# A hybrid decoder block: the products with w_out and w_up by Strassen's algorithm too, and h normalised with tokens on partitions

## The chip, the cores and the metric

The kernel runs on one core of a Trainium2 chip. The metric is the device time of one execution in microseconds (us); lower is better. Three executions of the kernel before took 1032.06, 1034.04 and 1034.89 us, with a median of 1034.04 us.

## The reference

One layer, 512 tokens, width 1024, float32. `u = rmsnorm(x)`, one wide projection of `u`, a gated DeltaNet branch and a forgetting-attention branch with 8 heads each, their outputs merged by two sigmoid gates, and then the part that the change touches:

```python
merged = jax.nn.sigmoid(gate_a) * y_a + jax.nn.sigmoid(gate_b) * y_b
h = x + merged @ w_out[l]                                            # 1024 x 1024

hn = rmsnorm(h, norm_mlp_g[l])
x = h + jnp.square(jax.nn.relu(hn @ w_up[l])) @ w_down[l]            # 1024 x 4096, 4096 x 1024
```

## The kernel before

**Precision.** Every large product is made of three TensorE matmuls: each operand is split into a rounded part hi and a rest lo, and hi·hi, hi·lo and lo·hi are added in PSUM.

**Weight units.** All weights come in units of 128 x 1024. `seq` lists them in the order of use. For each unit `prefetch_raw` issues the load (SP's queue), LA_RAW = 3 units ahead of the call that uses it, and `prefetch_split` makes two tiles of it, LA_SPLIT = 2 units ahead: ScalarE casts hi (L185), VectorE subtracts (lo = raw - hi, L186). The pool `whl` has four buffers for hi and four for lo, so a unit's cast can start only when TensorE has used the hi of the unit four places before it. For most weights a unit is one call of `dense` (L197 to L208), which makes 128 outputs for all 512 tokens: 16 matmuls of 128x512 with hi (L203, L204), then 8 with lo (L207).

**w_out and w_up before.** They are eight and 4 x 8 such calls. After each w_out unit VectorE adds x (L913: h, features on partitions); ScalarE and VectorE split h times the norm's gain, and square and sum it. The reciprocal root of the mean square is computed by two sets of small matmuls (`sumsq` L282, `inv_rms` L294), spread over the partitions as `rb_h`, and multiplied in only behind the product with w_up (`relu`, L951; ScalarE squares, L952). So no step of the norm stands between the products with w_out and w_up. 32 transposes (`tokens_first`, L935) give h with tokens on partitions for the sum of the output.

**w_down before.** The 4096 features are taken in four chunks, each w_up (8 units) and then w_down. w_down is multiplied by Strassen's algorithm in Winograd's form: seven products P1, P5, P6, P3, P7, P2, P4 of half-size blocks instead of eight, each of two units (s0, s1) of 12 matmuls 128x512 (L1015 to L1017). The sums of weight blocks are made by DMA: P1, P3 and P2 use blocks as they are, and P5 = P1 + block, P6 = P5 + block, P4 = P6 + block, P7 = P3 + block are accumulating transfers on GpSimd's queue into the same tile (L161). Such a transfer can start only when the older sum has been split: TensorE's next-but-one product hangs on a chain split, transfer, split, transfer. The sums of activation blocks are `act_forms`, made by VectorE (L974 to L980) and split by ScalarE and VectorE (`shi` L968, `slo` L969). VectorE adds the products to the accumulators (L992).

**The order.** The code is written in program order; a scheduler then puts the instructions into one in-order queue for each engine by priorities and its own estimate of times. An instruction whose input is late holds everything behind it on its engine.

Of the kernel before, what the change touches and what calls it, by code (L numbers as in the profile page):

```python
# [23 lines left out]
NPG = 34  # L24
# [3 lines left out]
NDRAW = 7  # L28
NWARM = 10
NZ1 = 5  # L30
LA_RAW = 3
LA_SPLIT = 2
INV_STEP = 2500


def hybrid_block(tc, a, out):
# [4 lines left out]
    up = ctx.enter_context(tc.tile_pool(name="up", bufs=1))  # L41
# [3 lines left out]
    pmm = ctx.enter_context(tc.tile_pool(name="pmm", bufs=NMM, space=PSUM))  # L45
    pat = ctx.enter_context(tc.tile_pool(name="pat", bufs=8 - NMM, space=PSUM))
    drp = ctx.enter_context(tc.tile_pool(name="drp", bufs=1, space=DRAM))
    mix = ExitStack()
    rwp = mix.enter_context(tc.tile_pool(name="rwp", bufs=3))
    atp = mix.enter_context(tc.tile_pool(name="atp", bufs=1))  # L50
    sbp = mix.enter_context(tc.tile_pool(name="sbp", bufs=1))
    fxp = mix.enter_context(tc.tile_pool(name="fxp", bufs=2))

# [17 lines left out]

    def const(shape, s, dt=F32):
        return cp.tile(shape, dt, tag=s, name=s)
# [56 lines left out]
    for i in range(KT):  # L130
        seq += [("w_gb", i), ("w_pf", i)]
    seq += [("w_o", i) for i in range(KT)]
# [4 lines left out]
    PRODUCTS = ("P1", "P5", "P6", "P3", "P7", "P2", "P4")  # L137
    for c in range(NC):
        seq += [("w_u", c * 8 + i) for i in range(8)]
        seq += [(p, (c, s_)) for p in PRODUCTS for s_ in range(NSUB)]  # L140
    raws, units = [], []
    pos = [0]

    FACTOR = {"P1": (0, None), "P5": (1, "P1"), "P6": (2, "P5"), "P3": (2, None), "P7": (1, "P3"), "P2": (3, None),
              "P4": (3, "P6")}
    factors = {}

    def prefetch_raw(n):
        while len(raws) < min(len(seq), n):
            nme, i = seq[len(raws)]
            if nme in PRODUCTS:
                q, old = FACTOR[nme]
                if old is None:
                    raw = draw.tile([P, D], F32, tag="draw", name=nm("draw"))
                    nc.sync.dma_start(raw, a["w_d"][i[0], q, i[1]])
                else:
                    raw = factors[old, i[1]]  # L160
                    nc.gpsimd.dma_start(raw, a["w_d"][i[0], q, i[1]], accum_op=ALU.add)  # L161
                factors[nme, i[1]] = raw
                raws.append((raw, [slice(0, D)]))
                continue
            w = 256 if nme == "w_ab" else D
            raw = wraw.tile([P, D], F32, tag="raw", name=nm("raw"))
            cuts = [slice(0, 512), slice(512, D)] if 0 < len(raws) < 3 else [slice(0, w)]
            for c in cuts:
                nc.sync.dma_start(raw[:, c], a[nme][i][:, c])
            raws.append((raw, cuts))  # L170
# [18 lines left out]
    def unit(nme):  # L189
        n = pos[0]  # L190
        assert seq[n][0] == nme, (seq[n], nme)
        pos[0] += 1
        prefetch_raw(n + 1 + LA_RAW)
        prefetch_split(n + 1 + LA_SPLIT)
        return units[n]
# [101 lines left out]
    uhi = up.tile([P, KT, T], F32R, tag="uhi", name="uhi")  # L297
    ulo = up.tile([P, KT, T], F32R, tag="ulo", name="ulo")
# [9 lines left out]
    def uh(k):  # L308
        return uhi[:, k, :]

    def ul(k):
        return ulo[:, k, :]
# [468 lines left out]
    def fox_pair(hp):  # L781
        vts = ([], [])
        for pn in range(3):
            us = [unit("w_fox"), unit("w_fox")]
            pg2 = [page(s="fqk"), page(s="fqk")]
            for t2 in range(2):
                ps = mmps("fx")
                for tb in (2 * t2, 2 * t2 + 1):
                    o = ps[:, (tb % 2) * 256:(tb % 2 + 1) * 256]
                    for k in range(KT):  # L790
                        w = us[k // 4][0][:, (k % 4) * 256:(k % 4 + 1) * 256]
                        mm(o, uhi[:, k, cs(tb)], w, start=(k == 0), stop=False)  # L792
                        mm(o, ulo[:, k, cs(tb)], w, start=False, stop=False)  # L793
                    for k in range(KT):
                        mm(o, uhi[:, k, cs(tb)], us[k // 4][1][:, (k % 4) * 256:(k % 4 + 1) * 256], start=False,  # L795
                           stop=(k == KT - 1))
# [97 lines left out]
    mg = []  # L894
    for n in range(KT):
        ps = dense("w_gb", uh, ul)
        sg = page(s="sg")
        act.activation(sg, ps, AF.Sigmoid)
        ps = dense("w_pf", lst(obs, 0), lst(obs, 1))
        vec.tensor_tensor(sg, ps, sg, op=ALU.mult)  # L900
        pool.tensor_tensor(sg, sg, ma[n], op=ALU.add)
        mg.append(split(sg))


    hT, hg = [], []
    hhi = up.tile([P, KT, T], F32R, tag="uhi", name="hhi")
    hlo = up.tile([P, KT, T], F32R, tag="ulo", name="hlo")
    sqs = page(s="sqs")
    for n in range(KT):
        xi = row_tile(a["xT"][n])  # L910
        ps = dense("w_o", lst(mg, 0), lst(mg, 1))
        xr = page(s="h")
        vec.tensor_tensor(xr, ps, xi, op=ALU.add)  # L913
        hT.append(xr)
        hg.append(split(xr, mlp_g[:, n:n + 1], dst=(hhi[:, n, :], hlo[:, n, :])))
        sq = page(s="sq") if n else sqs
        act.activation(sq, xr, AF.Square)
        if n:
            vec.tensor_tensor(sqs, sqs, sq, op=ALU.add)
    rs_h = const([P, NCH], "rs_h")  # L920
    rb_h = const([P, T], "rb_h")
    start(inv_rms(sumsq(sqs), rs_h, rb_h))


    mix.close()
    draw = ctx.enter_context(tc.tile_pool(name="draw", bufs=NDRAW))
    actp = ctx.enter_context(tc.tile_pool(name="actp", bufs=2))
    accs = [None] * 8

    def tokens_first():  # L930
        for tb in range(NCH):
            for l in range(2):
                pt = atps("hT")
                for n in range(4):
                    nc.tensor.transpose(pt[:, cs(n)], hT[4 * l + n][:, cs(tb)], ident)  # L935
                acc = page(s="acc")
                act.copy(acc, pt)
                accs[tb * 2 + l] = acc
                yield

    def mlp_up(c):
        forms = []
        for s_ in range(NSUB):
            blocks = []
            for j in range(2):
                blk = actp.tile([P, 2, T], F32, tag="act", name=nm("act"))
                for f in range(2):
# [4 lines left out]
                    act.activation(blk[:, f, :], r, AF.Square)  # L952
                blocks.append(blk)
            forms.append(act_forms(*blocks))
        return forms

    def halves(x):
        return v3(x[:, :], 2)

    def act_forms(b0, b1):  # L960

        h_ = T // 2
        a11, a21, a12, a22 = b0[:, :, :h_], b0[:, :, h_:], b1[:, :, :h_], b1[:, :, h_:]
        res = {}

        def put(p, x):
            hi, lo = page(F32R, "shi"), page(F32R, "slo")
            act.copy(halves(hi), x)  # L968
            vec.tensor_tensor(halves(lo), x, halves(hi).bitcast(F32), op=ALU.subtract)  # L969
            res[p] = hi, lo  # L970
# [125 lines left out]
```

## Time and profile before

| | |
|---|---|
| median of three runs | 1034.04 us (1032.06 to 1034.89) |
| the profiled execution | 1031.1 us, span 1029.3 us, granted clock 0.998 |
| TensorE busy | 1018.1 us, 99%, 5825 matmul records |
| VectorE, ScalarE, GpSimd busy | 620.7, 494.7, 183.0 us |
| w_out stage | about 655 to 692.9 us |
| first chunk: w_up, w_down | 692.9 to 742.1 with h's transposes, 742.1 to 780 |
| the MLP | 692.9 to 1029.3 us |

Times in the trace are from the start of the span. A "unit" below is one 128 x 1024 tile of weights.

### The profile page before, as it was taken

Reading aid. Unit: us, or ns where it says so; the run is one execution under the profiler, and the core shown is the slowest. Engines: PE = TensorE matmul, PEld = TensorE weight load, DVE = VectorE, ACT = ScalarE, POOL = GpSimd, SP = SyncE. Lnnn points to the kernel's source line nnn. Section 1 sums busy time; section 2 is a strip of 40 time slices with the busy share of each in tenths; the row PEclk is TensorE's granted clock in tenths of the full one; section 3 lists DMA queues with packets and bytes.
Section 4 is the critical chain, followed back from the end, with each engine's and each line's share of the span. In section 5 each row is a group of like instructions: output and inputs, shape, how many; then the busy total and the mean of one; then the engine's idle time right before and its main releaser. Section 6 shows DMA issues by size and latency. Waiting matters only on the chain.

```text
span 1029.3 us, 14835 instructions
## 1 busy us (share of the span) xinstructions
PE 1018.1 (99%) x5825; PEld 873.5 (85%) x5825; DVE 620.7 (60%) x1077; ACT 494.7 (48%) x742; POOL 183.0 (18%) x163
## 2 busy tenths in 40 slices
PE   9999999999999999999999999999999999999998
PEld 7788899998788999988888888888888888888886
DVE  6876777453667696354645333453685586577575
ACT  7765353445654554357753323344543453444442
POOL 1446130113441310203100112000110110020020
PEclk9999999999999999999999999999999999999999
DMA  6344223234233223124435333346475375375163
GB/s 217 139 124 154 92 62 96 66 98 144 82 108 110 88 75 93 52 93 133 155 111 177 100 102 99 117 123 225 85 174 171 86 144 200 96 129 186 40 112 114
DMA packets 54407, 122.86 MB, mean 119 GB/s; under 512 B 5729, under 2 KB 22337, under 8 KB 54337
## 3 DMA queue, kind: packets, MB, share of 16 engines
q1 hardware_dynamic: 49696, 105.12, 31.7%
q0 software_dynamic: 4640, 16.78, 9.5%
q8 instruction: 46, 0.75, 0.3%
q14 instruction: 25, 0.20, 0.1%
HBM read 113.45 MB, written 8.44 MB: 118 GB/s over the span
## 4 chain that ended last, share of the span: by engine, by line
PE 92%; DVE 3%; DMA 1%; issue 1%; POOL 1%; ACT 1%; SPq 0%; DVEq 0%; ACTq 0%; POOLq 0%
PE mm L203 16%; PE mm L204 16%; PE mm L207 16%; PE down L1015 5%; PE down L1016 5%; PE down L1017 5%; PE fx L795 5%; PE fx L792 4%; PE fx L793 4%; PE fo L775 2%; PE sc L750 2%; DMA row<-rowd 1%; PE pT L766 1%; PE v L639 1%; DVE conv L492 1%
## 5 line engine op out<-in xcount | busy, mean ns | idle before, releaser
L185 ACT CAST hi<-raw 128x1024 fp32r<-128x1024 f32 (+1 forms) x130 | 134.1, 1037 | 167.0 <-PE mm L204 114.6
L186 DVE TENSOR_TENSOR lo<-raw,hi 128x1024 fp32r<-128x1024 f32 (+1 forms) x130 | 160.7, 1239 | 74.6 <-PE mm L207 32.6
L203 PE MATMUL mm<-uhi,hi 128*128 128x512 f32 x344 | 136.4, 397 | 3.1 <-DVE conv L492 2.5
L204 PE MATMUL mm<-ulo,hi 128*128 128x512 f32 x344 | 136.5, 398 | 1.1 <-DVE ulo L218 1.1
L204 PE MATMUL mm<-hlo,hi 128*128 128x512 f32 x256 | 99.7, 389 | 0.0
L203 PE MATMUL mm<-hhi,hi 128*128 128x512 f32 x256 | 99.6, 390 | 0.0
L792 PE MATMUL fx<-hi,uhi 128*128 128x256 f32 x384 | 98.0, 290 | 0.3 <-DVE conv L492 0.3
L793 PE MATMUL fx<-hi,ulo 128*128 128x256 f32 x384 | 96.1, 286 | 0.0
L207 PE MATMUL mm<-uhi,lo 128*128 128x512 f32 x344 | 89.2, 395 | 0.0
L1017 PE MATMUL down<-lo,shi 128*128 128x512 f32 x224 | 87.2, 389 | 0.0
L1016 PE MATMUL down<-hi,slo 128*128 128x512 f32 x224 | 87.2, 389 | 0.0
L185 ACT CAST hi<-draw 128x1024 fp32r<-128x1024 f32 x56 | 57.9, 1049 | 60.7 <-DMA draw<-w_d 39.6
L1015 PE MATMUL down<-hi,shi 128*128 128x512 f32 x224 | 86.6, 389 | 0.0
L204 PE MATMUL mm<-lo,hi 128*128 128x512 f32 x207 | 80.3, 391 | 0.0
L203 PEld LDWEIGHTS mm<-uhi,hi 128*128 128x128 f32 x344 | 64.7, 188 | 18.4 <-issue 4.1
L203 PE MATMUL mm<-hi,hi 128*128 128x512 f32 x207 | 79.8, 391 | 0.0
L186 DVE TENSOR_TENSOR lo<-draw,hi 128x1024 fp32r<-128x1024 f32 x56 | 67.7, 1220 | 19.0 <-ACT hi L185 19.0
L204 PEld LDWEIGHTS mm<-ulo,hi 128*128 128x128 f32 x344 | 64.7, 188 | 15.3 <-DVE ulo L218 2.3
L161 POOL DMA_DIRECT2D draw<-w_d x32 | 28.0, 874 | 271.8 <-DVE lo L186 230.7
L207 PEld LDWEIGHTS mm<-uhi,lo 128*128 128x128 f32 x344 | 63.6, 188 | 13.2 <-issue 0.5
L792 PEld LDWEIGHTS fx<-hi,uhi 128*128 128x128 f32 x384 | 73.6, 192 | 1.2 <-issue 0.9
L793 PEld LDWEIGHTS fx<-hi,ulo 128*128 128x128 f32 x384 | 73.6, 192 | 0.5 <-issue 0.2
(297 smaller groups left out, 1942.8 us busy)
## 6 DMA issues: line engine op xcount, KB each, us to landing
raw<-w_u SPq DMA_DIRECT2D x32, 512.0 KB, 3.6
draw<-w_d POOLq DMA_DIRECT2D x32, 512.0 KB, 5.5
raw<-w_gdn SPq DMA_DIRECT2D x24, 512.0 KB, 3.6
raw<-w_fox SPq DMA_DIRECT2D x24, 512.0 KB, 3.6
draw<-w_d SPq DMA_DIRECT2D x24, 512.0 KB, 4.5
row<-rowd SPq DMA_DIRECT2D x24, 256.0 KB, 5.2
raw<-w_ga SPq DMA_DIRECT2D x8, 512.0 KB, 4.0
raw<-w_pg SPq DMA_DIRECT2D x8, 512.0 KB, 3.6
```

The lines of the kernel that those rows point to most:

```text
L161: nc.gpsimd.dma_start(raw, a["w_d"][i[0], q, i[1]], accum_op=ALU.add)
L185: act.copy(hi[:, c], raw[:, c])
L186: vec.tensor_tensor(lo[:, c], raw[:, c], hi[:, c].bitcast(F32), op=ALU.subtract)
L203: mm(o, w, rhi(k), start=(k == 0), stop=False)
L204: mm(o, w, rlo(k), start=False, stop=False)
L207: mm(o, lo[:, k * cols:(k + 1) * cols], rhi(k), start=False, stop=(k == KT - 1))
L792: mm(o, uhi[:, k, cs(tb)], w, start=(k == 0), stop=False)
L793: mm(o, ulo[:, k, cs(tb)], w, start=False, stop=False)
L795: mm(o, uhi[:, k, cs(tb)], us[k // 4][1][:, (k % 4) * 256:(k % 4 + 1) * 256], start=False, stop=(k == KT - 1))
L1015: mm(ps[tb], shi[:, t], wh, start=first and s_ == 0 and f == 0, stop=False, skip_group_check=True)
L1016: mm(ps[tb], slo[:, t], wh, start=False, stop=False, skip_group_check=True)
L1017: mm(ps[tb], shi[:, t], wl, start=False, stop=last, skip_group_check=True)
```

## The change

w_out and w_up are multiplied by the same seven products as w_down. The order of the products is set for each by `ORDER`; `FACTOR` says which weight sum is made from which.

- **w_out:** `tokens_product`, the function that w_down uses as well (matmuls at L1017 to L1019): 14 units of 12 matmuls 128x512 instead of 8 units of 24. The merged activations are put by quarters for that, with their forms. Tokens now stand on partitions in the result; it is added to accumulators that were loaded with x (L996).
- **h's norm:** `normalise_h`, for 256 tokens at a time: ScalarE squares with a running sum (L1049), VectorE adds, GpSimd raises to the power, VectorE scales each token (L1059), 32 transposes (L1065), and ScalarE puts the gain on and writes the quarters `hq` (L1069). Their seven forms are made once and used by all four chunks.
- **w_up:** 14 units in each chunk instead of 8, each of 24 matmuls 128x256 (L1118) instead of 24 of 128x512. Its products are added, cut at zero and squared on ScalarE and VectorE (L1124 to L1146, L1099).
- **Weight sums:** eight accumulating transfers on GpSimd's queue for w_out and eight for w_up in each chunk, as for w_down (72 in all instead of 32; the line is L168 now). `prefetch_new` loads plain blocks up to 6 units ahead.
- **Around it:** w_gb's eight units and then w_pf's, instead of one by one in turn. More pages (50), 12 accumulator pages, three buffers for the weight blocks of s0 (those of the plain loads) and three for s1 (seven in one pool before), and all eight PSUM banks in one pool from there on. The four buffers for hi and lo stay.

The core of the diff:

```diff
+    ORDER = {"w_o": ("P1", "P5", "P6", "P2", "P3", "P7", "P4"), "w_u": ("P1", "P2", "P5", "P6", "P3", "P7", "P4"),
+             "w_d": ("P1", "P5", "P6", "P3", "P7", "P2", "P4")}
+    FACTOR = {"P1": (0, None), "P2": (3, None), "P5": (1, "P1"), "P6": (2, "P5"), "P3": (2, None), "P7": (1, "P3"),
+              "P4": (3, "P6")}
...
+            if old is None:
+                raw = fresh[s_].tile([P, D], F32, tag="raw", name=nm("draw"))
+                nc.sync.dma_start(raw, a[w][c, q, s_])
+            else:
+                raw = factors[old, i]
+                nc.gpsimd.dma_start(raw, a[w][c, q, s_], accum_op=ALU.add)
...
-    for n in range(KT):
-        xi = row_tile(a["xT"][n])
-        ps = dense("w_o", lst(mg, 0), lst(mg, 1))
-        xr = page(s="h")
-        vec.tensor_tensor(xr, ps, xi, op=ALU.add)
...
-    start(inv_rms(sumsq(sqs), rs_h, rb_h))
...
+    def normalise_h(i):
+        sl = slice(2 * i, 2 * i + 2)
+        with tc.high_priority(offset=AHEAD):
+            for l in (0, 1) if i == 0 else (1, 0):
+                for t in range(2):
+                    junk = page(s="junk")
+                    act.activation(junk, accs[2 * i + t][l], AF.Square, accum_out=ss_h[:, 2 * i + t, l:l + 1])
+            vec.tensor_tensor(rs_h[:, sl], ss_h[:, sl, 0], ss_h[:, sl, 1], op=ALU.add)
+            vec.tensor_scalar(rs_h[:, sl], rs_h[:, sl], 1.0 / D, EPS, op0=ALU.mult, op1=ALU.add)
+            rsq(rs_h[:, sl], rs_h[:, sl])
...
+    tokens_product("w_o", 0, mgens, mforms, h_done)
...
-                    ps = dense("w_u", lst(hg, 0), lst(hg, 1))
-                    tick()
-                    r = page(s="relu")
-                    vec.scalar_tensor_tensor(r, ps, 0.0, rb_h, op0=ALU.max, op1=ALU.mult)
...
+                for f in range(2):
+                    o = of_half(ps, f)
+                    for part, wx in ((0, whi), (1, whi), (0, wlo)):
+                        for kb in range(4):
+                            mm(o, wx[:, (2 * kb + f) * P:(2 * kb + f + 1) * P], of_half(hforms[p, kb // 2][part], kb % 2),
```

**ScalarE's queue at the middle of the first w_down.** The names: `hi` is a weight unit's cast, `shi` the cast of an activation form. In before, from the cast of P6's first unit on: `shi` 7138 is P3's second form, `hi` 7270 is P7's first unit.

```order
L185 CAST hi_1303_7196<-draw_1265_7020 128x1024 [waits DMASW3_49,PE_49]
L968 CAST shi_1283_7128<-s_1282_7126 128x512 [waits DVE_49]
L185 CAST hi_1306_7214<-draw_1271_7055 128x1024 [waits DMASW4_49,PE_49]
L968 CAST shi_1285_7133<-s_1282_7126 128x512 [waits DVE_49]
L185 CAST hi_1309_7234<-draw_1305_7212 128x1024 [waits DMAHW4_49,PE_49,Activation_49]
L185 CAST hi_1311_7251<-draw_1308_7232 128x1024 [waits DMAHW6_49,PE_49,Activation_49]
L968 CAST shi_1287_7138<-s_1282_7126 128x512 [waits DVE_49]
L968 CAST shi_1289_7143<-act_1259_6985 128x512
L968 CAST shi_1291_7147<-act_1270_7054 128x512 [waits Activation_49]
L968 CAST shi_1293_7151<-act_1270_7054 128x512
L185 CAST hi_1313_7270<-draw_1305_7212 128x1024 [waits DMASW7_49,PE_49,Activation_49]
```

The same place now, from P6's first unit (`hi` 8265); `shi` 8196 is P5's second form, `shi` 8258 P3's second, `hi` 8357 P7's first unit.

```order
L203 CAST hi_1491_8265<-draw_1453_7997 128x1024 [waits DMASW3_49,PE_49]
L947 CAST shi_1471_8196<-s_1470_8194 128x512 [waits DVE_49]
L947 CAST shi_1473_8201<-s_1467_8188 128x512 [waits DVE_49]
L203 CAST hi_1493_8281<-draw_1456_8031 128x1024 [waits DMASW4_49,PE_49]
L203 CAST hi_1500_8311<-draw_1479_8213 128x1024 [waits DMAHW6_49,PE_49]
L947 CAST shi_1475_8206<-s_1470_8194 128x512 [waits DVE_49]
L203 CAST hi_1503_8330<-draw_1482_8232 128x1024 [waits DMAHW7_49,PE_49]
L947 CAST shi_1485_8253<-s_1467_8188 128x512 [waits DVE_49]
L203 CAST hi_1509_8357<-draw_1479_8213 128x1024 [waits DMASW7_49,PE_49,Activation_49]
L947 CAST shi_1487_8258<-s_1470_8194 128x512 [waits DVE_49]
```

P5's second form stands right behind P6's first weight cast, which waits for an accumulating transfer (DMASW), in both. P3's second form stood ahead of P7's first weight cast and now stands behind it.

**TensorE's queue at the same place, now.** `down` 8262 and 8263 are P5's banks, 8210 and 8211 P6's; `hi` 8234 is P5's second unit.

```order
L1017 MATMUL down_1489_8262<-hi_1483_8234,shi_1471_8196 128x512 [waits Activation_49]
L1017 MATMUL down_1490_8263<-hi_1483_8234,shi_1471_8196 128x512
L1017 MATMUL down_1477_8210<-hi_1491_8265,shi_1473_8201 128x512 [waits DVE_49,Activation_49]
L1018 MATMUL down_1489_8262<-hi_1483_8234,slo_1472_8197 128x512 [waits DVE_49]
L1019 MATMUL down_1489_8262<-lo_1484_8235,shi_1471_8196 128x512
L1018 MATMUL down_1490_8263<-hi_1483_8234,slo_1472_8197 128x512
```

Before, P6's matmuls began only behind P5's last. Now one of P6's stands between P5's matmuls, ahead of the first with `slo` 8197, and the queue waits there for ScalarE and for VectorE.

**ScalarE's queue at the end of w_out, now.** `hnT` are the transposes of normalised h, `hq` its quarters, `acc` 6459 and 6461 rows of h of the second 256 tokens, `shi` 6767 and 6811 the two halves of the first form, which w_up's first unit uses.

```order
L1069 ACTIVATE hq_1178_6471<-hnT_1245_6760,c_norm_mlp_g_157 128x256 [waits PE_49]
L947 CAST shi_1246_6767<-hq_1178_6471 128x512 [waits Activation_49]
...
L203 CAST hi_1281_6899<-draw_1240_6738 128x1024 [waits DMAHW5_49,PE_49]
L1049 ACTIVATE junk_1279_6890,ss_h_6480<-acc_1174_6459 128x512 [waits DVE_49]
L1069 ACTIVATE hq_1182_6475<-hnT_1255_6804,c_norm_mlp_g_157 128x256 [waits PE_49]
L1069 ACTIVATE hq_1182_6475<-hnT_1255_6804,c_norm_mlp_g_157 128x256
L1049 ACTIVATE junk_1280_6892,ss_h_6480<-acc_1176_6461 128x512 [waits DVE_49]
L947 CAST shi_1256_6811<-hq_1182_6475 128x512 [waits Activation_49]
```

None of these rows was there before, where the casts of h (L217) stood one behind each w_out unit. Two squares of the last rows of h now stand ahead of the second half of the first form.

More of the change, by code (lines that the diff above doesn't have):

```diff
@@ L142, in hybrid_block @@
+    raws, units = {}, []
     pos = [0]
[L147 to L148 removed]
     factors = {}
[L151 to L170 removed]
+    fresh = [None, None]
```

353 lines of the change are left out of this document (237 added, 116 removed).

## The prediction

> **What bounds the kernel now.** First the page: which engine is full, and whether it is full everywhere.
>
> ```profile
> span 1029.3 us, 14835 instructions
> PE 1018.1 (99%) x5825; PEld 873.5 (85%) x5825; DVE 620.7 (60%) x1077; ACT 494.7 (48%) x742; POOL 183.0 (18%) x163
> PE   9999999999999999999999999999999999999998
> PEclk9999999999999999999999999999999999999999
> PE 92%; DVE 3%; DMA 1%; issue 1%; POOL 1%; ACT 1%; SPq 0%; DVEq 0%; ACTq 0%; POOLq 0%
> ```
>
> TensorE is busy in every slice at full clock, and 92% of the chain that ended last is its own. The list of TensorE's waits says how little it waits:
>
> ```profile
> PE mm L203 <- DVE conv L492: 2.5, 3, 1.5
> PE warm L233 <- DVE expo L228: 1.1, 1, 1.1
> ```
>
> The longest single wait is 1.5 us. So matmuls taken away count at their full price, and every new wait counts too. The other engines have room in the stages that change (w_out, the first w_up, the first w_down):
>
> ```profile
> core 0: us, PE busy (x) PEld busy (x) DVE busy (x) ACT busy (x) POOL busy (x), PEclk, DMA share, GB/s
> 655.00:692.90 37.90, 37.90 (x169) 31.39 (x168) 21.02 (x27) 16.95 (x22) 0.00 (x0) 1.00 0.42 132
> 692.90:736.40 43.50, 43.50 (x217) 36.56 (x216) 21.51 (x31) 20.70 (x32) 2.85 (x3) 1.00 0.50 162
> 736.40:774.50 38.10, 38.10 (x170) 31.55 (x169) 29.50 (x37) 16.94 (x21) 5.20 (x6) 1.00 0.73 159
> ```
>
> **What the change takes from TensorE.** A matmul costs its pitch in a full stream, not its recorded duration (pipelined ones overlap). Two stretches of TensorE's timeline give both widths:
>
> ```profile
> 800.10 1.98 PE L207 MATMUL mm<-hhi,lo 128*128 128x512 f32 x8
> ...
> 805.54 1.98 PE L207 MATMUL mm<-hhi,lo 128*128 128x512 f32 x8
> ```
>
> ```profile
> 210.43 1.12 PE L795 MATMUL fx<-lo,uhi 128*128 128x256 f32 x8
> 211.39 0.28 PE L792 MATMUL fx<-hi,uhi 128*128 128x256 f32 x1
> ```
>
> One w_up unit of 24 wide matmuls takes 805.54 - 800.10 = 5.44 us, 226.7 ns each. Eight half-wide ones take 211.39 - 210.43 = 0.96 us, 120 ns each: half the width at 53% of the price.
>
> - w_out: 8 x 24 = 192 matmuls become 14 x 12 = 168, all wide: 24 x 0.2267 = **-5.4 us**.
> - w_up: 4 x 8 x 24 = 768 wide become 4 x 14 x 24 = 1344 half-wide: 174.1 to 161.3, **-12.8 us**. Strassen's eighth would be 21.8; the half-wide matmuls give 9 of it back.
> - The norm's small matmuls go, the transposes stay 32:
>
> ```profile
> L294 PE MATMUL rb<-ident,rs_h 128*128 128x128 f32 x8 | 1.1, 274 | 0.0
> L282 PE MATMUL ss<-ones,sqs 128*128 128x64 f32 x8 | 1.0, 268 | 0.0
> ```
>
> 16 of them, 2.1 us busy with some overlap: **-1.9 us**. Together **-20.1 us** if nothing new waits.
>
> The Trainium skill (TensorE: Matmul & The Clock Gate, "Back-to-back issue gap") gives an isolated gap of 262 cycles at 256 columns and 518 at 512, a ratio of 1.98 where the rows have 1.89. By those figures w_up would save about 19 us, and the forecast below would be 6 us lower; the rows decide.
>
> **What it adds beside TensorE.** Per chunk six more weight splits (1.05 on ScalarE, 1.22 on VectorE) and the adds and squares of w_up's products by quarters. VectorE's 51 us in a chunk's two stages (21.5 + 29.5 above) grow by some 7, to about 58 of 78 us; ScalarE less. Both hide, and if that cover were gone the seven would cost at most 7 a chunk. What does not hide by load can still wait by order.
>
> **First new wait: from w_up to w_down, in each of the four chunks.** Here are ScalarE's, TensorE's and VectorE's timelines around the first w_down of before; its start, 742.08, is the zero of the times below.
>
> ```profile
> 724.14 1.05 ACT L185 CAST hi<-draw 128x1024 fp32r<-128x1024 f32 x1 [0.43 <-PE mm L204]
> ...
> 745.35 1.05 ACT L185 CAST hi<-draw 128x1024 fp32r<-128x1024 f32 x1 [1.72 <-DMA draw<-w_d]
> 746.31 0.61 ACT L968 CAST shi<-s 128x512 fp32r<-128x512 f32 x1
> ...
> 760.52 1.05 ACT L185 CAST hi<-draw 128x1024 fp32r<-128x1024 f32 x1 [3.82 <-DMA draw<-w_d]
> ```
>
> ```profile
> 742.08 0.39 PE L1015 MATMUL down<-hi,shi 128*128 128x512 f32 x1
> ...
> 750.69 0.39 PE L1016 MATMUL down<-hi,slo 128*128 128x512 f32 x1
> ...
> 763.84 0.39 PE L1015 MATMUL down<-hi,shi 128*128 128x512 f32 x1
> ```
>
> ```profile
> 746.44 1.23 DVE L186 TENSOR_TENSOR lo<-draw,hi 128x1024 fp32r<-128x1024 f32 x1 [1.01 <-ACT hi L185]
> 747.58 0.68 DVE L969 TENSOR_TENSOR slo<-s,shi 128x512 fp32r<-128x512 f32 x1
> ...
> 761.60 1.23 DVE L186 TENSOR_TENSOR lo<-draw,hi 128x1024 fp32r<-128x1024 f32 x1 [2.37 <-ACT hi L185]
> ```
>
> P1's first cast starts at -17.9, when TensorE is done with the hi of the unit four places before: four units of 5.44 ahead, less the part that still reads hi. From there split, accumulating transfer, split, transfer lead to P6's first cast at +3.3 (745.35), behind which, on ScalarE's queue, stands the cast of P5's second form (746.31); its rest is ready on VectorE at +6.2 (747.58 + 0.68). TensorE asks for that at 750.69, +8.6: 2.4 us to spare. P7's first rest is ready at 762.83 and needed at 763.84: 1.0 to spare.
>
> Now the units ahead last 24 x 0.120 = 2.88 us. The same buffer is free four units ahead less 20/24 of one: 4 x 2.88 - 2.4 = 9.1 us before w_down. The chain from there, with the landing time of the accumulating transfers:
>
> ```profile
> DMA to landing us min/median/max: 5.3/5.5/6.5
> ```
>
> Cast and rest 2.3, so -6.8; issue 0.3 and landing 5.5, -1.0; cast and rest, +1.3; 0.4 and 5.5, P6's first cast at +7.2. That is 3.9 later than before, against 2.4 to spare: 1.5 late. In the new order an accumulator's add stands between P6's rest and P5's on VectorE, 0.6 more. **About 2.1 us late.** ScalarE's queue holds P5's form and P6's; VectorE's holds the adds that free P6's bank; TensorE waits for both.
>
> Then P7: its chain starts from P3's split, which hangs on buffers in the same way as before, so its cast comes near +18.4 to 20 again. In the new order P3's second form stands behind that cast on ScalarE, not ahead of it. TensorE wants it at about +19.5, or +21.6 with the lateness so far; cast 1.05, form 0.6 and rest 1.3 (with the weight's rest ahead) give +21.4 to 23. **0 to 1.5 more; I take 1.2.**
>
> Per chunk 3.3, four times: **+13.2 us** (4 x 2 = 8 at 5.3 us of landing and no second wait, 4 x 5.3 = 21 at 6.5 us).
>
> **Second new wait: from w_out to w_up, once.** No step of the norm stood there; now TensorE needs h's last sums squared, rooted, scaled, transposed and split. No row shows this chain; its parts have rows:
>
> ```profile
> L763 DVE TENSOR_SCALAR p<-p,fsm 128x512 f32<-128x512 f32 x8 | 4.7, 583 | 0.2
> L276 POOL TENSOR_TENSOR rs_h<-rs_h,expo 128x4 f32<-128x4 f32 x1 | 1.0, 1017 | 49.5 <-DVE rs_h L289 49.5
> L917 ACT ACTIVATE sq<-h 128x512 f32<-128x512 f32 x7 | 4.3, 617 | 0.0
> ```
>
> The first 256 tokens are done after P3, with P7 and P4 (10.9 us of TensorE) behind. Two adds (1.2), two squares (1.2 to 1.6), sums 0.3, power 1.0, scaling 0.6: 4.4 to 4.8, and up to 3 more if the adds stand behind the weight splits of P7 and P4, which wait for transfers. The first transposes stand ahead of P4, 5.4 after P3: **0 to 2.3, I take 1.** At w_out's end ScalarE has two squares of the last rows ahead of the second half of the first form. After the last matmul: 0.4, add 0.6, square 0.8, quarters 0.7, square 0.8, form 0.6, rest 0.7 = 4.6, while TensorE has 10 transposes or matmuls, 1.2 us, of other work: **3.4.** Forms of P5 and P6 in the first w_up stand behind weight casts that wait for transfers: **0 to 2, I take 1.** Together **+5.4 us** (3 to 8).
>
> Inside w_up P5 is two products behind P1, and P6 one behind P5: 17.3 us from w_up's start to P6, in which the chain (9.1 ahead at most) ends near +7; I cost it at nothing, and up to 1 us a chunk if transfers collide. w_out, the new order of w_gb and w_pf, and the accumulators' loads likewise, within 2 us.
>
> **Sum.** -20.1 + 13.2 + 5.4 = -1.5: the profiled execution's 1031.1 becomes 1029.6. The median of the runs lies 2.9 above it, so **1032.5 us**. By the bounds, -20.1 + 8 + 3 and -20.1 + 21 + 8, this case's own range is 1025 to 1043. A difference under 0.3% (3.1 us) can hardly be measured, so I forecast no change.
>
> **Rivals.**
>
> *A. All hidden.* Transfers land by the time of need, because the scheduler orders by its own estimate and a TensorE queue that waits at one place has forms in stock at the next. For: in before the same chain cost nothing. Against: its spare 2.4 us is less than the 3.9 that are lost. 1034.0 - 20.1 = 1014.
>
> *B. The short wait only.* P7's lateness hides behind P5's, and w_out's seam shrinks to 1: -20.1 + 8.4 + 1 = -10.7, 1023.
>
> *C. Slower: transfers crowd.* 72 accumulating transfers instead of 32, and the DMA share, 0.73 in w_down, rises in w_up. Its place is the chain into each w_down, where two landings stand in a row ahead of P6 and one ahead of P7. From a median landing of about 6.0 the chain becomes the bound. At 6.5 each wait grows by 1 to 2 a chunk and the chain in w_up shows: +3 x 4 = 12, 1045. For: when three transfers overlapped before, one took 6.3:
>
> ```profile
> 754.18 0.87 POOL L161 DMA_DIRECT2D draw<-w_d  x1 [0.87 <-DVE lo L186]
> ```
>
> (issued 754.18, its cast released at 760.52). Against: the median of 5.5.
>
> The Trainium skill (same page, "HAM oscillation — how this bites in real kernels") says that TensorE idle for over about 3.4 us comes back at half clock until it has been busy as long. No run here shows it, since no wait was over 1.5 us. By it the seam of w_out alone could lose 2 to 3 us more.
>
> **How the numbers follow.** The forecast's case has 0.42, as the chain is read from rows but rests on one landing time: 0.22 within 0.3%, 0.10 to each side. A 0.20, B 0.18 (both faster), C 0.20 (slower). Faster 0.48, same 0.22, slower 0.30. The likeliest single case is still the one near zero; its time is the prediction. The range leaves out the lower half of A and the upper half of C: 1014 to 1047.
>
> **What would show it.** Right: TensorE's waits name `shi` and `slo` at w_down's P5 and P3 with 2 to 4 us in each chunk, and the forms of h with 3 to 4 us once; the w_up matmuls have a pitch of 120 ns; VectorE stays under 75%. Wrong: a TensorE without waits in w_down (A), a landing over 6 us (C), a w_up pitch other than 120 ns, or waits in w_gb to w_out, which I cost at nothing.

## The result, and the profile after

The changed kernel takes 1060.43 us in the median of four runs (1058.83 to 1064.7), against 1033.05 us (1031.86 to 1034.89) for the kernel before: a ratio of 1.027, 95% interval 1.0235 to 1.0305. It is slower by 27 us, where the forecast was 1032.5 us and the range ended at 1047.

The page of the changed kernel:

```profile
span 1058.6 us, 16239 instructions
PE 1015.5 (96%) x6361; PEld 887.9 (84%) x6361; DVE 671.7 (63%) x1136; ACT 558.0 (53%) x855; POOL 219.2 (21%) x212
PE   8999999999999999999999999989899899989888
DMA  6344222134243231325354347757868688778783
PE 55%; issue 19%; DMA 14%; DVE 7%; POOL 4%; ACT 2%; SPq 0%; POOLq 0%; ACTq 0%; DVEq 0%
q0 software_dynamic: 10400, 37.76, 20.8%
```

TensorE is still busy for 96% of the span, and reads as full in most slices. But the chain that ended last is TensorE's for 55% only, where it was 92%: 14% of it now are transfers. The DMA row has mostly sixes to eights in the last 40%, where before ones to sevens stood. GpSimd's own queue (q0) moved 37.76 MB and kept the 16 engines for 20.8% of the span.

TensorE's waits (in us: total, times, longest):

```profile
PE down L1017 <- ACT shi L947: 12.7, 12, 2.0
PE down L1017 <- ACT hi L203: 5.5, 4, 2.7
PE up L1118 <- ACT shi L947: 4.4, 3, 3.0
PE down L1017 <- DVE acc L996: 2.5, 4, 0.7
PE hnT L1065 <- DVE proj L1059: 2.2, 1, 2.2
PE down L1018 <- DVE slo L948: 2.1, 3, 1.2
```

Those are the waits that the prediction named: forms (`shi`, `slo`) in w_down, the first form of w_up behind w_out, h's transposes. New is the wait on `hi`, the cast of w_down's first weight unit, four times. Together they are 29.4 us. By stage, windows of the changed kernel (the second chunk's w_up and w_down; columns as in the prediction's windows):

```profile
789.90:825.00 35.10, 34.75 (x289) 34.51 (x288) 17.99 (x20) 19.98 (x28) 5.18 (x6) 1.00 0.79 166
832.50:878.50 46.00, 40.67 (x168) 31.15 (x167) 36.76 (x48) 23.86 (x32) 6.90 (x8) 0.96 0.74 160
```

and the same w_down in the kernel before:

```profile
823.70:861.80 38.10, 38.10 (x169) 31.52 (x168) 31.06 (x38) 17.24 (x21) 4.37 (x5) 1.00 0.78 189
```

w_down takes 46.0 us (and 0.8 us of its matmuls that stand ahead of w_up's end) where it took 38.1. 5.3 us of it TensorE is idle; and its granted clock is 0.96, so that matmuls take longer too. The DMA engines are busy for 0.74 of it and move 160 GB/s, where 0.78 moved 189 before.

The time by stages, in us, from where the matmuls of the stage ahead end in TensorE's timeline; w_out starts at 649.6 in both kernels (before, "about 655" above is a unit too late). The third column is what the matmuls cost by the prediction's pitches.

| stage | before | by the matmuls | after |
|---|---|---|---|
| w_out, first w_up, all transposes | 92.5 | 82.2 | 92.7 |
| first w_down | 38.1 | 38.1 | 47.6 |
| second chunk | 81.6 | 78.4 | 88.5 |
| third chunk | 81.6 | 78.4 | 87.2 |
| last chunk, to the end | 85.9 | 82.7 | 93.0 |

The losses over the third column are 10.5, 9.5, 10.1, 8.8 and 10.3 us, 49.2 in all; less the 20.1 that the matmuls give, 29.1. The spans differ by 29.3. TensorE's waits from w_out on are 30.3 of the 49.2; the rest is taken up under "Why the prediction was wrong".

### The profile page after: what moved, and what is told of

It reads as the page before. It is cut to its first block, busy times and chain, and to the rows that moved or that the text cites. A ratio compares the mean times of both kernels' runs of the same rounds, so it can differ in the third digit from the quotient of the medians.

```text
span 1058.6 us, 16239 instructions
## 1 busy us (share of the span) xinstructions
PE 1015.5 (96%) x6361; PEld 887.9 (84%) x6361; DVE 671.7 (63%) x1136; ACT 558.0 (53%) x855; POOL 219.2 (21%) x212
## 3 DMA queue, kind: packets, MB, share of 16 engines
q0 software_dynamic: 10400, 37.76, 20.8%
## 4 chain that ended last, share of the span: by engine, by line
PE 55%; issue 19%; DMA 14%; DVE 7%; POOL 4%; ACT 2%; SPq 0%; POOLq 0%; ACTq 0%; DVEq 0%
PE mm L222 9%; PE mm L223 9%; PE mm L226 8%; DMA draw<-w_d 7%; PE fx L813 4%; DMA draw<-w_u 4%; PE fx L810 4%; PE fx L811 4%; DVE lo L204 2%; POOL draw L168 2%; PE fo L793 2%; PE sc L768 2%; DMA row<-rowd 1%; PE down L1018 1%; ACT hi L203 1%
## 5 line engine op out<-in xcount | busy, mean ns | idle before, releaser
L204 DVE TENSOR_TENSOR lo<-draw,hi 128x1024 fp32r<-128x1024 f32 x126 | 153.9, 1224 | 108.1 <-ACT hi L203 108.0
L203 ACT CAST hi<-draw 128x1024 fp32r<-128x1024 f32 x126 | 130.9, 1046 | 163.9 <-DMA draw<-w_d 57.0
L204 DVE TENSOR_TENSOR lo<-raw,hi 128x1024 fp32r<-128x1024 f32 (+1 forms) x90 | 111.8, 1247 | 87.5 <-PE mm L226 53.7
L203 ACT CAST hi<-raw 128x1024 fp32r<-128x1024 f32 (+1 forms) x90 | 91.9, 1029 | 110.4 <-PE mm L223 81.2
L1017 PE MATMUL down<-hi,shi 128*128 128x512 f32 x280 | 107.7, 407 | 21.6 <-ACT shi L947 12.7
L1018 PE MATMUL down<-hi,slo 128*128 128x512 f32 x280 | 112.4, 405 | 2.8 <-DVE slo L948 2.1
L1019 PE MATMUL down<-lo,shi 128*128 128x512 f32 x280 | 109.1, 398 | 0.0
L1017 PEld LDWEIGHTS down<-hi,shi 128*128 128x128 f32 x280 | 52.4, 192 | 40.8 <-ACT shi L947 23.0
L1118 PE MATMUL up<-shi,hi 128*128 128x256 f32 x448 | 73.8, 286 | 4.4 <-ACT shi L947 4.4
L226 PEld LDWEIGHTS mm<-uhi,lo 128*128 128x128 f32 x344 | 63.7, 188 | 13.2 <-issue 0.5
L1118 PE MATMUL up<-slo,hi 128*128 128x256 f32 x448 | 73.7, 285 | 0.0
L1118 PE MATMUL up<-shi,lo 128*128 128x256 f32 x448 | 73.0, 285 | 0.0
L1018 PEld LDWEIGHTS down<-hi,slo 128*128 128x128 f32 x280 | 54.1, 193 | 18.7 <-DVE slo L948 7.9
```

The costliest lines, as they stand in the source:

```text
L203: act.copy(hi[:, c], raw[:, c])
L204: vec.tensor_tensor(lo[:, c], raw[:, c], hi[:, c].bitcast(F32), op=ALU.subtract)
L226: mm(o, lo[:, k * cols:(k + 1) * cols], rhi(k), start=False, stop=(k == KT - 1))
L1017: mm(ps[t], shi[:, k], wh, start=first and s_ == 0 and f == 0, stop=False, skip_group_check=True)
L1018: mm(ps[t], slo[:, k], wh, start=False, stop=False, skip_group_check=True)
L1019: mm(ps[t], shi[:, k], wl, start=False, stop=last, skip_group_check=True)
```

## The experiments

A time given without a range is that of a single execution. Those of the kernel before lie between 1029.7 and 1034.9 us, so a few us are not read from a single one. Line numbers shift by the lines that a version adds, so that L1017 of the change can be L1018 to L1024 below. A diff shows the lines that matter; "..." stands for others. "A chunk" is the second chunk, from its first w_up matmul to that of the third: 81.6 us before, 88.5 after, 78.4 by the matmuls.

Three theories. **1:** the chain of split and transfer into w_down starts too late, since short w_up units free the hi buffers late. **2:** the accumulating transfers crowd and land late. **3:** the forms are late because ScalarE's and VectorE's in-order queues hold them behind other work.

**P2 second in w_down**

```diff
-             "w_d": ("P1", "P5", "P6", "P3", "P7", "P2", "P4")}
+             "w_d": ("P1", "P2", "P5", "P6", "P3", "P7", "P4")}
```

> Theory 1 (the chain starts too late): the chain split, transfer, split, transfer into each w_down starts only some 8 us ahead, since w_up's short units free the hi buffers late; each step then misses its product. With P2 second, P5, P6 are wanted 5.4 us later and the chain's times stay: the waits at P5 and P6 go, that at P3 and P7 stays. w_down's stage 40 to 42 us instead of 45 to 47, the whole about 1040 us. Theory 2 (transfers crowd): 72 accumulating transfers remain, with a landing near 6.7 us when two overlap, and what P5 gains P7 and P4 lose: w_down 44 us or more, the whole over 1050 us.

1048.58 us, a chunk 87.0. Of the waits on forms in w_down one of 0.9 us is left, but the waits on `hi` grow:

```profile
PE down L1017 <- ACT hi L203: 10.1, 6, 2.7
```

Between the two theories: the deadlines of P5 and P6 mattered, and part of what they gained was lost at the next place.

**Two products between each sum and the next**

```diff
+             "w_d": ("P1", "P2", "P5", "P3", "P6", "P7", "P4")}
...
-        for p in ORDER[w]:
+        for p in ORDER["w_u"] if w == "w_d" else ORDER[w]:
```

> Two products (10.9 us) between each sum and the sum made of it everywhere in w_down. Theory 1: no wait inside w_down but perhaps the one at its first cast; stages of 38.5 to 40 us, the whole about 1030 us. Theory 2: as for P2 second, over 1050 us. Theory 3 (ScalarE's and VectorE's queues cannot keep up with units of 2.7 us, transfers or not): waits on forms stay, over 1050 us.

1068.86 us, slower than the change. The largest wait shows a fault of the experiment:

```profile
PE down L1017 <- DVE acc L996: 15.2, 4, 4.0
```

P6 and P7 add into the same PSUM banks, and next to each other P7 must wait until VectorE has read P6's sum. So its time tells nothing about the theories. The other waits in w_down are 7.4 us on `hi` and 4.5 on `shi`.

**w_up dense again, the rest of the change kept**

```diff
-        seq += product_units("w_u", c) + product_units("w_d", c)
+        seq += [("w_u", c * 8 + i) for i in range(8)] + product_units("w_d", c)
...
```

> w_up as before (8 units of 24 wide matmuls in a chunk), the rest of the change kept. Theory 1: the units ahead of w_down last 5.44 us again, so w_down's stages are back at 38 to 39 us without waits. Theory 3: forms are still made late, w_down 44 us or more. The seam from w_out to w_up is dearer here, 10 to 14 us, since the first unit needs all of h; the whole about 1040 us by theory 1, over 1060 by theory 3.

1033.97 us, a chunk 81.6 as before, no wait in w_down; the seam behind w_out 7.2 us:

```profile
PE hnT L1064 <- DVE proj L1058: 7.2, 2, 4.7
```

So the new form of w_down's code and forms is not late by itself. Both what w_up's units do (short) and what its transfers do (32 more) are gone here, so theories 1 and 2 stay.

**No weight sums**

```diff
-            q, old = FACTOR[nme]
+            q, old = FACTOR[nme][0], None
...
```

> Leaves out the weight sums of all three products: each product uses one plain block, loaded by SP up to six units ahead; all matmuls, splits and forms stay. Theories 1 and 2: without the chain w_up's stages are 40 to 41 us and w_down's 38 to 39, the whole about 1020 us. Theory 3: w_down stays at 45 us, the whole over 1050 us.

1019.76 us, a chunk 79.2. All but 0.8 us of the loss in a chunk is the sums': theory 3 falls in its plain form, since splits, forms, adds and their queues are all there.

**No weight sums in w_up alone**

```diff
+            old = None if w == "w_u" else old
...
```

> Leaves out the weight sums of w_up alone (plain blocks, loaded ahead by SP); w_out's and w_down's chains stay, 40 accumulating transfers instead of 72, and w_up's units stay short. If the chain into w_down starts too late because of the short units alone (theory 1), w_down's stages stay at 44 to 47 us and the whole at about 1048 us. If w_up's transfers crowd it and delay its first cast (theory 2), w_down comes to 39 to 41 us and the whole to 1025 to 1030 us. Both together would give something between, about 1037.

1040.06 us, a chunk 83.5. From the second chunk on w_up runs without a wait and w_down's first cast is in time; w_down still waits for forms:

```profile
PE down L1018 <- ACT shi L948: 7.2, 7, 1.3
```

About half of a chunk's loss comes from w_up's own transfers, half from w_down's eight behind short units.

**Five buffers**

```diff
-    whl = ctx.enter_context(tc.tile_pool(name="whl", bufs=4))
+    whl = ctx.enter_context(tc.tile_pool(name="whl", bufs=5))
...
```

> Five buffers for hi and for lo instead of four, splits asked for three units ahead and loads four: P1's cast can start 2.9 us earlier, the transfers are as many. Theory 1: some 2.5 us of the 8 in each w_down go, the whole about 1050 us. Theory 2: no change within 4 us.

1063.1 us, a chunk 90.1. The chain did come earlier: at the second w_down, which starts at 831.35, P5's first cast stands at -0.4 us and P6's at +7.9, where the change has +1.8 and +10.2. But nothing came of it. ScalarE's casts moved ahead, where they wait for transfers, and w_up's last quarter and P5's first form stand behind P6's, so that TensorE waits 5.0 us for that form:

```profile
839.22 1.04 ACT L203 CAST hi<-draw 128x1024 fp32r<-128x1024 f32 x1 [3.12 <-DMA draw<-w_d]
840.17 0.59 ACT L1143 ACTIVATE act<-up 128x512 f32<-128x512 f32 x1
840.66 0.61 ACT L947 CAST shi<-s 128x512 fp32r<-128x512 f32 x1
```

An earlier start alone gives no time. Theory 1 is not settled by that, since the order on ScalarE changed with it.

**P1 early**

```diff
-        seq += product_units("w_u", c) + product_units("w_d", c)
+        pu, pd = product_units("w_u", c), product_units("w_d", c)
+        k = NSUB * (ORDER["w_u"].index(EARLY) + 1)
+        seq += pu[:k] + pd[:NSUB] + pu[k:] + pd[NSUB:]
...
```

> w_down's product P1 is moved ahead to stand behind w_up's P6 (it needs only the first quarter of the activations), everything else in the old order: P1's split comes 17 us earlier relative to P5, and the chain to P5 and P6 has three more products of lead. Theory 1: the waits at w_down's P1, P5 and P6 go, those at P3 and P7 stay at 1 to 2 us: the whole 1030 to 1036 us. Theory 2: as many transfers in the same time, the whole over 1048 us.

`EARLY` is P6. 1063.41 us, a chunk 89.7. But for 0.2 us on a rest, one wait a chunk is left in w_down, and it is as long as all of them:

```profile
PE down L1020 <- ACT shi L950: 25.8, 4, 7.3
```

P5's form needs w_up's last quarter, and P1 had covered its making.

**P1 early and P2 next**, the edits of P1 early and of P2 second together:

> P1 behind w_up's P6 and P2 the first product behind w_up, then P5 P6 P3 P7 P4. P1 early alone waits 7 us a chunk for P5's form, which needs w_up's last quarter: nothing stood between. With P2 between, 5.4 us of that are covered and the wait on P1's cast of P2 second is gone too: the whole 1034 to 1042 us. If the transfers' rate is the bound, over 1048.

1047.54 us, a chunk 83.2: with P2 as the cover the longest wait for that form is 1.7 us. The expected 1034 to 1042 was missed by 5 us; w_up now waits up to 2.2 us at a time for VectorE's adds of its products.

**The norm left out**

```diff
+    vec.memset(rs_h, 1.0)
...
-                    act.activation(junk, accs[2 * i + t][l], AF.Square, accum_out=ss_h[:, 2 * i + t, l:l + 1])
...
-            rsq(rs_h[:, sl], rs_h[:, sl])
```

> Leaves out the norm's sums of squares and the root (the scale is a constant 1); adds, scaling, transposes and forms stay. If the squares and the root are what w_up waits for behind w_out, the two waits there (2.2 and 3.0 us) and the slow matmuls behind them go, 6 to 8 us, the whole about 1053. If the wait is for the adds, the transposes and the casts in their queues, less than 3 us go.

1058.56 us. The wait of h's transposes and that of w_up's first form go, and one of 3.1 us stands two products later, on another form: the seam is a chain of adds, transposes and casts in their queues, and the norm is not what makes it long, as far as one execution shows.

**The casts' order forced**

```diff
+            pn, pi = seq[len(units) - 1] if units else (None, None)
+            if pn in FACTOR and (pn, pi[2]) in formtab.get(pi[:2], ()):
+                act.copy(hi[:, 0:1], formtab[pi[:2]][pn, pi[2]][0][:, 0:1])
...
```

> The change, but each weight cast of w_down is made to follow the cast of the form of the product unit before it (a copy of one column from that form into the tile that the cast overwrites). Theory 3 now reads: TensorE waits for forms only because their casts stand in ScalarE's in-order queue behind weight casts that wait for accumulating transfers. Then the waits on shi in w_down, 4 to 5 us a chunk, shrink to what the weights themselves are late, 1 to 2 us, and the slow matmuls behind them with it: 4 to 6 us a chunk, the whole about 1040 us. If the transfers themselves are the bound (theory 2), the wait moves to the weights and the whole stays over 1054 us.

1060.33 us, a chunk 88.0. The wait changes its name and hardly its size:

```profile
PE down L1021 <- ACT hi L207: 14.5, 12, 2.8
PE down L1021 <- ACT shi L951: 5.1, 3, 2.0
```

Theory 3 gains nothing in its second form either: with the forms ahead, the weights themselves are late. How late they were without the forced order, this run doesn't say, since a cast held back by it comes later too. On top of two of the other orders the forced order made them slower, by 8 and 18 us, where a gain or no change was expected.

> P2 second in w_down, with the same forced order of casts. P2 second alone took 1048.6. Theory 3: the forms were no longer late there, so little more to gain, 1044 to 1049 us; the waits left are on P1's cast, 2.5 us, which the transfers of w_up's P7 and P4 delay (theory 2).

1056.18 us.

> The same with the forced order of casts as well: if P5's form still waits behind a weight cast, 1 to 2 us a chunk more go, the whole 1028 to 1036 us; otherwise as without it.

1065.48 us.

**The transfers without their addition**

```diff
-                nc.gpsimd.dma_start(raw, a[w][c, q, s_], accum_op=ALU.add)
+                nc.gpsimd.dma_start(raw, a[w][c, q, s_])
```

> Leaves out the addition: the 72 transfers on GpSimd's queue overwrite the older block instead of adding to it; every wait, queue and buffer stays as in the change. If the extra work of an accumulating transfer (it reads what it adds to, and several in flight land after 8 to 9 us) is what makes the chain late, the landing comes to about 4 us, most waits in w_down go, the whole 1025 to 1035 us. If the chain of split, issue, transfer and buffers is late with any transfer, the whole stays over 1048 us.

1018.09 us, below the expected range, and a chunk 78.5: the matmuls' own price to 0.1 us, with every link, queue and buffer in place. The landing times of these transfers and their queue:

```profile
DMA to landing us min/median/max: 3.6/3.9/5.0
```

```profile
q0 software_dynamic: 10400, 37.76, 11.9%
```

and the change's, which adds:

```profile
DMA to landing us min/median/max: 5.3/5.7/9.0
```

The same 37.76 MB cost 20.8% of 1058.6 us of the 16 engines with the addition and 11.9% of 1016.4 us without: 220 against 121 us, 1.8 times. This settles the main question: the addition in the transfers costs the 42 us. (GpSimd's longer issue, 862 ns against 527 ns, is part of it.)

**P5's sum in a tile of its own**

```diff
-            if old is None:
+            if old is None or nme == "P5":
...
+                if nme == "P5":
+                    nc.gpsimd.dma_start(raw, a[w][c, q, s_], accum_op=ALU.add)
...
```

> P5's sum gets a tile of its own: P1's block is loaded a second time and P5's is accumulated on it at once, so that it no longer hangs on P1's split (18 more plain transfers of 512 KB). If the links of the chain are the bound, P5 and P6 are ready 8 us earlier, the waits in w_down's first half go, the whole about 1040 us. If the DMA engines are the bound in these stages, the added traffic makes it no faster, 1056 us or more.

1060.29 us, a chunk 89.5. The pool of plain blocks of s1 has six buffers instead of three here. One link less in the chain and 18 plain loads more: no gain. In w_down the waits on `shi` are 10.9 us in all, against 12.7.

**Loads beside plain transfers**

```diff
-                nc.gpsimd.dma_start(raw, a[w][c, q, s_], accum_op=ALU.add)
+                nc.gpsimd.dma_start(raw, a[w][c, q, s_])
+                nc.sync.dma_start(fresh[2].tile([P, D], F32, tag="raw", name=nm("spare")), a[w][c, q, s_])
...
```

> plain_chain again (the 72 transfers overwrite instead of adding), and with each of them one more plain load of the same 512 KB on SP's queue into a spare tile that nobody reads, so that the DMA engines are as busy as in the change. If their total load is the bound, the transfers of the chain land after 5 to 7 us again, the waits come back, the whole over 1045 us. If the long landing of the accumulating transfer itself is, whatever else the engines do, the chain's transfers stay near 4 to 4.5 us and the whole at 1017 to 1024 us.

1031.17 us, between the two. SP ran far ahead with the spare loads, so that the load was not spread as meant: from 630 to 750 us the DMA engines were busy for 0.89, where the change has 0.72, and then it was gone.

```profile
630.00:750.00 120.00, 110.86 (x653) 96.72 (x652) 92.30 (x122) 71.93 (x118) 23.66 (x30) 1.00 0.89 337
```

```profile
DMA to landing us min/median/max: 3.8/7.4/9.2
```

The same window without the spare loads:

```profile
630.00:750.00 120.00, 115.98 (x677) 102.64 (x676) 100.11 (x132) 78.58 (x125) 24.39 (x33) 0.99 0.52 168
```

```profile
DMA to landing us min/median/max: 3.7/3.9/4.9
```

Where plain transfers land as late as 7.4 us in the median, TensorE loses 5.1 us of work in that window. So lateness can be had without the addition, by load. But load does not make a plain transfer more work: q0's share is 11.6% of 1029.5 us here, 119 us, as without the spare loads. So what the change's transfers take beyond that, up to 220 us, is the addition's own. Whether the late landings in the change's stages come more from each addition's own length or from the load that the additions make together stays open.

**w_out alone by Strassen's algorithm.** h is transposed from the accumulators without the norm, the norm is multiplied in behind w_up as before, w_up is dense:

```diff
...
+                half(ps, hl, [4, 5, 6, 7], True, False)
...
+                half(ps, hl, [0, 1, 2, 3], False, True)
...
```

> A version after the runs so far: only w_out by Strassen's algorithm. w_up dense as before, the norm multiplied in behind it as before; h is transposed from the accumulators without the norm, and the first two w_up units start with the half of h that is done first. TensorE loses 24 matmuls, 5.4 us; the seam should cost 1 to 4 us instead of 12, the rest as before: 0.1 to 0.4% faster than before.

1032.93 us (1030.94 to 1035.17, twelve runs) against 1033.08: a ratio of 1.0001, interval 0.9989 to 1.0012. The 5.4 us are given back at the seams, in waits (1.1 us at w_out's start, 0.5 for h's transposes, and the one below) and in one stretch of 3.4 us at half clock from 694.4 on:

```profile
PE up L1102 <- ACT hhi L1055: 2.1, 1, 2.1
```

**w_up's sums by VectorE**, with P2 second in w_down and PSUM banks of its own for P4:

```diff
+                if old is not None:
+                    vec.tensor_tensor(raw, raw, factors[old, i], op=ALU.add)
...
```

> What the runs point to: w_up's weight sums are made by VectorE from blocks that SP loads plainly (8 adds of 1.2 us a chunk, VectorE has 15 us to spare there), so that only w_down's 32 and w_out's 8 transfers accumulate; in w_down P2 comes second, and P4 gets PSUM banks of its own, so that P7 and P4 need not wait for each other's adds. w_up's stages 40.3 us without waits, w_down's 39 to 41: 1026 to 1034 us. If VectorE's adds hold up its queue, w_up waits on its rests and the whole stays over 1040.

1054.33 us, ratio 1.0209 (1.0185 to 1.0234), a chunk 85.1. From the second chunk on w_up waits no more; w_down waits late, behind P3, for weight casts:

```profile
PE down L1019 <- ACT hi L205: 12.9, 8, 2.3
```

> The same with w_down's P1 behind w_up's P6, which gives the chain to P5 and P6 8 us more: if w_down still waits in dve_sums for P5 or P6, 1 to 2 us a chunk less, 1022 to 1030 us; if it waits for forms (P1 no longer stands between w_up and P2), no gain.

1044.63 us (1042.38 to 1052.03), ratio 1.0108 (1.0081 to 1.0135). P1 early gains 10 us here. Both expectations were missed. In the trace of the first version 24.5 us are lost against the kernel before: 2.0 ahead of w_out, 10.7 in w_out and the first w_up, 11.8 from the first w_down on. So w_down's own 32 sums behind short units keep about half of the loss. The seam behind w_out keeps nearly as much: TensorE waits there up to 4.6 us for h's transposes and 1.4 to 2.3 us for forms. What makes the seam longer than the change's was not tested. No version that makes all the sums beat the kernel before.

## Why the prediction was wrong

**The matmuls' sum was right.** -20.1 us by pitches of 226.7 and 120 ns: with plain transfers a chunk takes 78.5 us, where those pitches give 78.4. By the Trainium skill's isolated gap of 262 cycles at 2.4 GHz (TensorE: Matmul & The Clock Gate, "Back-to-back issue gap") the 336 matmuls of w_up in a chunk would take an estimated 36.7 us. With plain transfers they take 40.3 (41.0 from w_up's first matmul to the start of w_down, less three of w_down's). The trace has a longer gap than the page there.

**The places were right.** TensorE waits at w_down's P5 and P3 on forms, and behind w_out on h's. (One reading was off without weight: the matmul at 763.84 in before uses P7's cast, and its rest is first used at 764.29, so that 1.5 us were to spare and not 1.0.)

**The step that failed is the first new wait, "Per chunk 3.3, four times: +13.2 us", and with it "Inside w_up ... I cost it at nothing".** The loss was 8.8 to 10.1 us a chunk, 38.7 in all. The chain's own rows show three reasons. GpSimd's transfers and ScalarE's casts at the second w_down, which starts at 832.5:

```profile
803.53 0.86 POOL L168 DMA_DIRECT2D draw<-w_u  x1 [4.65 <-DMA draw<-w_u]
...
809.64 0.86 POOL L168 DMA_DIRECT2D draw<-w_u  x1 [0.57 <-DVE lo L204]
827.44 0.86 POOL L168 DMA_DIRECT2D draw<-w_d  x1 [16.93 <-DVE lo L204]
829.58 0.86 POOL L168 DMA_DIRECT2D draw<-w_d  x1 [1.27 <-DVE lo L204]
```

```profile
818.58 2.00 ACT L203 CAST hi<-draw 128x1024 fp32r<-128x1024 f32 x2 [2.75 <-DMA draw<-w_u]
...
824.86 1.03 ACT L203 CAST hi<-draw 128x1024 fp32r<-128x1024 f32 x1
...
834.27 1.05 ACT L203 CAST hi<-draw 128x1024 fp32r<-128x1024 f32 x1 [5.05 <-DMA draw<-w_d]
...
836.70 1.05 ACT L203 CAST hi<-draw 128x1024 fp32r<-128x1024 f32 x1 [0.22 <-DMA draw<-w_d]
...
838.14 0.61 ACT L947 CAST shi<-s 128x512 fp32r<-128x512 f32 x1
...
842.69 1.04 ACT L203 CAST hi<-draw 128x1024 fp32r<-128x1024 f32 x1 [3.41 <-DMA draw<-w_d]
```

- In w_up four transfers (P7's and P4's) are issued within 6.1 us. In the window around them the landing goes up to 8.9 us. ScalarE waits for them until 818.58, and w_down's first cast comes at 824.86, 7.6 us ahead of w_down and not 9.1.
- w_down's first two transfers are issued 2.1 us apart and overlap: 827.44 to the cast at 834.27 is 6.8 us, where I put 5.8 for issue and landing. P5's first cast comes at +1.8 and not -1.0, P6's at +10.2 and not +7.2.
- P5's own first form (838.14) stands behind P5's second cast (836.70), so TensorE waits for it as well; I had counted the wait at P5's second half only.

So the chain starts 1.5 us late, its first link is 1 us longer than I put it, and the lateness begins in w_up. Rival C named that mechanism ("72 accumulating transfers instead of 32 ... two landings stand in a row") and priced it at 12 us; the runs show it to be the main one, at more than twice that price. It got a chance of 0.20, with the median of 5.5 us as the reason against; the median after is 5.7, only 0.2 higher. The median hides it: landings go up to 9.0 us where transfers overlap, and those are the ones in the chain. Rival A ("all hidden") is refuted by the rows above, B by their size.

**The slow matmuls were left out of the sum.** After a wait of 2.0 us in w_down TensorE's matmuls come at half the pace for a while:

```profile
844.30 1.05 PE L1017 MATMUL down<-hi,shi 128*128 128x512 f32 x2 [2.02 <-ACT shi L947]
845.73 0.77 PE L1017 MATMUL down<-hi,shi 128*128 128x512 f32 x1 [0.38 <-DVE acc L996]
846.29 0.74 PE L1018 MATMUL down<-hi,slo 128*128 128x512 f32 x1
846.83 0.63 PE L1019 MATMUL down<-lo,shi 128*128 128x512 f32 x1
...
848.04 0.39 PE L1017 MATMUL down<-hi,shi 128*128 128x512 f32 x1
```

The starts lie 0.43 to 0.56 us apart instead of 0.227. In the trace's clock record this is one stretch of 3.41 us at half clock. Five of them stand behind w_out's start, one in the first w_up and one in each w_down, and their starts lie whole multiples of 3.41 us apart. At 1.7 us each they are about 8.5 of the 49.2 us. The prediction mentioned the Trainium skill's rule for that (TensorE: Matmul & The Clock Gate, "HAM oscillation — how this bites in real kernels", idle for over about 3.4 us) and put 2 to 3 us on the seam of w_out alone. Here the trace differs from it: waits of 1.8 to 2.4 us in all, within the 3.41 us ahead, were enough, in one piece or in two. The length of a single wait does not decide. One of 2.16 us, up to 685.76, was followed by full pace; it lies across two of those stretches, with 1.65 us in the second. That stretch, the one ahead of the slow matmuls above, and what follows each (columns as in the windows above, the clock third from the end):

```profile
684.11:687.52 3.41, 1.76 (x9) 1.49 (x10) 2.54 (x7) 1.58 (x2) 0.71 (x1) 1.00 0.80 258
687.52:690.93 3.41, 3.41 (x21) 2.88 (x20) 3.41 (x6) 2.01 (x4) 0.90 (x1) 1.00 0.50 67
841.12:844.53 3.41, 1.39 (x7) 0.85 (x6) 1.12 (x2) 1.84 (x3) 0.00 (x0) 1.00 0.98 189
844.53:847.94 3.41, 3.03 (x7) 1.79 (x7) 3.41 (x6) 2.23 (x3) 0.86 (x1) 0.50 0.33 44
```

With 30.3 us of waits this makes 38.8 of the 49.2 us. Each of the 28 waits also costs some 0.16 us more than its row says, 4.5 in all, since a matmul's record (0.39 us) is longer than its pitch (0.227). About 6 us have no row.

**The second new wait was too small, +5.4 against 10.5 us.** Its three waits came as worked out: 2.2 us for the transposes (I took 1), 3.0 for the first form's second half (3.4), 0.7 and 0.8 for forms in the first w_up (1). On top came the half clock behind the 3.0 us, 0.9 us at w_out's start for the merged activations, and 0.2 us at w_up's end for w_down's first cast.

## What to carry to other kernels

A product that is saved costs what its operands cost: count the links between one use of an operand and the next, price each link by the transfers that will overlap there, not by the median of a calmer stage, and set the sum against the shortened time between the uses. An addition made by a transfer is work of the DMA engines, 1.8 times that of the plain transfer here. Before more of it is planned, look at their busy share in the stage beside the rate: here 0.74 to 0.79 at 160 to 166 GB/s, where plain transfers moved 185 to 192 at about 0.6.

## What the runs showed of the hardware

- An accumulating transfer of 512 KB lands after 5.3 us at best, a plain one from the same queue after 3.6; over the kernel the 72 took 1.8 times the DMA engines' time of plain ones. GpSimd's issue is longer too, 862 ns against 527 ns in the median.
- With several in flight they land after up to 9.0 us.
- TensorE's clock was halved for 3.41 us at a time, on a fixed grid of 3.41 us. In the changed kernel, from w_out to the last matmul, each halving followed a stretch of that grid with 1.8 to 2.4 us of waiting, and no stretch with 1.65 us or less was followed by one. In the other runs the line there lies between 1.5 and 1.85 us. One halving does not fit: at 408 us, in both kernels, where small 32x32 matmuls run and no wait is recorded.
- Half-wide matmuls (128x256) hold their pitch of 120 ns over the whole w_up, 1344 of them.
